# First matrix of the last MLP: seven products of block sums for eight

## The chip, the cores and the metric

The kernel runs on one core of a Trainium2 chip. The metric is the device time of one execution in microseconds (us); three runs of the kernel before took 1508.21, 1509.25 and 1509.27 us, so the median is 1509.25 us.

## The reference, cut to what matters

A model of two layers works on 16 meta tokens and 512 tokens of width 1024, in float32. Each layer has a token mixer and an MLP; only the MLP of the second layer is touched:

```python
def sq_relu_mlp(h, w1, w2):
    a = jax.nn.relu(h @ w1)
    return (a * a) @ w2
...
        hn = rms_norm(h, norm_g[l, 2])
        h = h + rms_norm(sq_relu_mlp(hn, mlp_w1[l], mlp_w2[l]), norm_g[l, 3])
    return h[:, N_META:]
```

`w1` is 1024 x 4096 and `w2` 4096 x 1024. In the second layer the MLP sees the 512 tokens only, since the meta tokens are dropped from the output.

## The kernel before, in words

**Float32 by three products.** Every operand of a large product is held as two parts of type float32r: `hi`, a copy in that type, and `lo`, what is left. `three` (L528) issues three matmuls for one k tile of 128 rows: hi hi, hi lo, lo hi. All of them are issued by `mm` (L140), so every matmul has line 140; the instructions of VectorE, ScalarE and GpSimd all come from the wrapper at line 88, and every DMA of the SP queue from line 147.

**Weights.** Weights come in chunks of 1 MB: for the first matrix 1024 rows by 256 columns. `fetch` asks for a chunk on SP's queue (two raw buffers), `prepare` splits it (ScalarE makes `wh`, VectorE `wl`, as two operations of 128x1024 each; three buffers for each of `wh` and `wl`), and `chunk` hands it to a product after preparing the next one and fetching the one after. The order of chunks is the list `plan`.

**The last MLP.** `Stream` holds the input: `st.hs` the stream itself, feature-major (8 tiles of 128 features by 512 tokens), and `half_of` its hi and lo parts times the norm's weights, by halves of 256 tokens. D_FF is worked off in four passes of 1024 (`q`). In each pass `mlp_in` makes 8 tiles of the squared ReLU from four chunks of the first matrix, and then four chunks of the second matrix are multiplied, with tokens on the output's partitions (`gemm_tok`); `out_tokens` adds the passes up in `ys`. In the first pass the leading two chunks are worked off by `gemm_lead`, one half of the tokens after the other, while the residual stream is just being made (`residual`); the other 14 chunks go through `gemm_full` (two output tiles of 128, 8 k tiles, three matmuls of 512 columns: 48 matmuls a chunk), and `relu2` evacuates a PSUM bank: ScalarE takes ReLU and square (hi), VectorE squares again and subtracts (lo). PSUM is used in pairs of banks, of which there are three for products (`pair`).

**The token-major stream.** The output needs the stream with tokens on partitions. `by_tokens`, a side task, transposes `st.hs` on TensorE during the first pass and keeps the eight tiles `ht` in SBUF until `finish` adds them.

**What sets the order.** TensorE's and ScalarE's instructions and the DMAs on SP's queue run in the order in which the program writes them. VectorE's and GpSimd's are put in order by the framework's planner, from a simulated timeline (`unpin`). Side tasks are generators: `spawn` gives one a due time on a clock that counts matmul columns, and `tick`, called between matmuls, runs the step that has waited longest. All small tiles come from one pool of 61 units of 128x528 (`U`).

Of the kernel before, what the change touches and what calls it, by code (L numbers as in the profile page):

```python
# [10 lines left out]
F32 = mybir.dt.float32  # L11
F32R = mybir.dt.float32r
# [61 lines left out]
def trunk(ctx, tc, io, out, dbg=None):  # L74
# [3 lines left out]
    class Engine:  # L78
        """an engine whose instructions keep the order they are written in where pinned is set"""
# [69 lines left out]
    # ------------------------------------------------------------ constants  # L149
# [16 lines left out]
    # ------------------------------------------------------------ input  # L166
# [47 lines left out]
    # ------------------------------------------------------------ accurate small functions  # L214
# [29 lines left out]
    def small_parameters():  # L244
# [13 lines left out]
        # softplus(-lam) * 4  # L258
# [13 lines left out]
        # softmax over the layers, its first row  # L272
# [9 lines left out]
    def s5_parameters():  # L282
        """S5: discretised transition, its powers, and z = (abar - 1) / a"""
# [61 lines left out]
        # nre = 1 - Re(abar), a_re = -ea  # L345
# [23 lines left out]
    # ------------------------------------------------------------ side work, interleaved with the main products  # L369
# [18 lines left out]
    def due():  # L388
        """the step of the side work that has waited longest, of those that have what they wait for"""
        return min((e for e in sides if e[2] is None or e[2]()), key=lambda e: e[0], default=None)  # L390

    def tick():
        """such a step if its time has come, and another where work is late"""
        for late in pace[1:]:
            e = due()
            if e and e[0] <= clk[0] - late:
                run(e)
# [8 lines left out]
    # ------------------------------------------------------------ weight stream  # L406
# [3 lines left out]
    def weights(w, r0, c0, kt=KT, eng=None, order=""):  # L410
        """order: which of rows (r) and columns (c) come as S5 has its features, in each tile (c g) for (g c)"""
        plan.append((w, r0, c0, kt, eng, order))

    def halves(n, kt):
        """the first chunks come in two parts"""
# [15 lines left out]

    def fetch(i):
        while state["dma"] <= min(i, len(plan) - 1):
            n = state["dma"]
            w, r0, c0, kt, _, order = plan[n]
            cw = CW * KT // kt
            raw = pr.tile([P, kt, cw], F32, tag="raw", name=nm("raw"))
# [11 lines left out]
    def prepare(i):  # L449
        fetch(i)  # L450
        while state["split"] <= min(i, len(plan) - 1):
# [48 lines left out]
    for l in range(2):  # L500
# [13 lines left out]
        for q in range(4):  # L514
            for i in range(4):
                weights(w1s[l], 0, q * D + CW * i)
# [11 lines left out]
    def three(o, wc, k, j, x, a, b):  # L528
        """one k tile of w^T x in three products of float32r parts"""
# [14 lines left out]
    def gemm(ps, wc, j, xs, cut, first=True, last=True, k0=0, n=KT):  # L544
        """accumulates w^T xs for the columns of cut in a PSUM pair"""
# [7 lines left out]
    def gemm_tok(o, wc, xs, c0, n, ks=range(KT), k0=0):  # L553
        """accumulates xs^T w for a block of columns of xs; w starts with k tile k0"""
# [9 lines left out]
    def meta_parts(xs):  # L564
        """hi and lo of the meta tokens side by side, as one stationary operand for each k tile"""
# [7 lines left out]
    def gemm_meta(o, wc, xm):  # L573
        """xs^T w for the meta tokens: what hi gives above what lo gives with the high part of w"""
# [7 lines left out]
    def meta_rows(u):  # L582
        """a side task: adds the two parts"""
# [5 lines left out]
    def gemm_full(ps, wc, j0, xs, c0, n=KT):  # L589
        """w^T xs for two tiles of w and 512 columns, a PSUM bank for each tile"""  # L590
# [6 lines left out]
    def gemm_wide(pss, wc, xs, cut, n=KT, j0=0):  # L597
        """two tiles and their halves side by side, for operands whose last tiles come late"""
# [6 lines left out]
    def split_halves(i):  # L605
        """the split of chunk i in two parts, the k tiles of its first half first"""
# [9 lines left out]
    def gemm_lead(chunks, xs, cut, ready, evac, early=None, lag=5.0):  # L616
        """two chunks, one half of the columns after the other, each tile of xs used as soon as it is there"""
# [3 lines left out]
        for h in range(2):  # L621
# [7 lines left out]
            for i in range(2):  # L629
                if i == len(wcs):  # L630
# [12 lines left out]
    def gemm_trail(parts, cut, evac, after):  # L643
        """the last chunks, one half of the columns after the other, so that what follows can start on the first"""
# [37 lines left out]
    # ------------------------------------------------------------ norms  # L682
# [1291 lines left out]
```

## Time and profile before

| | us |
|---|---|
| median of three runs | 1509.25 |
| span of the profiled execution, first to last instruction | 1506.2 |
| TensorE busy | 1452.0 |
| VectorE busy | 869.8 |
| ScalarE busy | 565.8 |
| GpSimd busy | 509.9 |

The profile is of one execution; its own time is known as the span, and the median of the runs is 3.05 us longer than that. PE is TensorE, DVE VectorE, ACT ScalarE, POOL GpSimd, SP the engine that issues the DMAs. A matmul's listed duration contains its way through the array, so the distance between starts tells the rate. The last MLP's first product starts at 1129.3 us, and its last matmul at about 1497 us.

### The profile page before, as it was taken

To read this page: it belongs to the slowest core of one execution; us is meant where nothing else is said; L and a number is where in the kernel's file an instruction comes from. 1 tells how busy PE (TensorE), PEld (TensorE's weight loads), DVE (VectorE), ACT (ScalarE), POOL (GpSimd) and SP (SyncE) were. 2 spreads that over 40 slices of the span, in tenths; PEclk is the share of its full clock that TensorE was granted. 3 is DMA by queue.
4 is the path that set the end of the run, shared out by engine and by line. 5 is a ranking of instruction groups with operands and counts; after the bars stand their busy time and mean duration, and the time that the engine had idled before them with its cause. 6 is when DMAs were issued, how large, how long until landed. Compare 5 with 4: busy or idle time off the path is not lost.

```text
span 1506.2 us, 24782 instructions
## 1 busy us (share of the span) xinstructions
PE 1452.0 (96%) x10216; PEld 1346.0 (89%) x10216; DVE 869.8 (58%) x1321; ACT 565.8 (38%) x935; POOL 509.9 (34%) x627
## 2 busy tenths in 40 slices
PE   7999998999999999999999889998999999999997
PEld 6998898889989999999999889988798888888887
DVE  5787699664279635345344937659469424334245
ACT  6344373443227222233233532344436324133133
POOL 3535264232122985629401444435123000000004
PEclk9999999999999999999999999999999999999999
DMA  7315012303155343423344285630142222413121
GB/s 245 100 57 156 29 61 73 107 33 132 61 149 161 99 148 114 137 84 107 121 135 166 86 194 189 170 86 29 57 154 67 102 84 84 140 56 132 64 84 56
DMA packets 154464, 162.38 MB, mean 108 GB/s; under 512 B 30292, under 2 KB 126912, under 8 KB 154336
## 3 DMA queue, kind: packets, MB, share of 16 engines
q1 hardware_dynamic: 151824, 160.23, 33.5%
q8 instruction: 80, 1.31, 0.3%
q10 hardware_dynamic: 2176, 0.52, 0.2%
q14 instruction: 32, 0.26, 0.1%
q0 software_dynamic: 352, 0.05, 0.0%
HBM read 136.89 MB, written 20.64 MB: 105 GB/s over the span
## 4 chain that ended last, share of the span: by engine, by line
PE 78%; DVE 15%; ACT 3%; issue 2%; DMA 1%; POOL 1%; SPq 0%; DVEq 0%; ACTq 0%; POOLq 0%
PE m L140 43%; PE wo L140 6%; PE v L140 4%; PE trail L140 3%; PE lead L140 3%; DVE wl L88 2%; PE gt L140 2%; PE av L140 2%; DVE m L88 2%; PE i L140 2%; PE f L140 2%; DVE z L88 1%; PE hs L140 1%; PE ms L140 1%; DVE rt L88 1%
## 5 line engine op out<-in xcount | busy, mean ns | idle before, releaser
L88 DVE TENSOR_TENSOR wl<-raw,wh 128x1024 fp32r<-128x1024 f32 (+1 forms) x204 | 265.8, 1344 | 82.3 <-ACT wh L88 81.7
L88 ACT CAST wh<-raw 128x1024 fp32r<-128x1024 f32 (+1 forms) x228 | 219.1, 1016 | 81.4 <-PE m L140 54.3
L140 PE MATMUL m<-nh,wh 128*128 128x264 f32 (+1 forms) x672 | 216.7, 323 | 0.0
L140 PE MATMUL m<-nl,wh 128*128 128x264 f32 (+1 forms) x672 | 215.6, 321 | 0.0
L140 PE MATMUL m<-nh,wl 128*128 128x264 f32 (+1 forms) x672 | 215.3, 320 | 0.0
L88 DVE TENSOR_TENSOR mr<-mr 128x528 f32<-128x528 f32 (+3 forms) x72 | 48.0, 668 | 184.3 <-ACT ah L88 183.0
L140 PEld LDWEIGHTS m<-nh,wh 128*128 128x128 f32 x672 | 126.4, 188 | 10.4 <-issue 0.7
L140 PEld LDWEIGHTS m<-nh,wl 128*128 128x128 f32 x672 | 126.4, 188 | 9.6
L140 PEld LDWEIGHTS m<-nl,wh 128*128 128x128 f32 x672 | 126.5, 188 | 9.3
L140 PE MATMUL m<-ah,wh 128*128 128x264 f32 x448 | 128.3, 286 | 0.0
L140 PE MATMUL m<-al,wh 128*128 128x264 f32 x448 | 127.3, 284 | 0.0
L140 PE MATMUL m<-ah,wl 128*128 128x264 f32 x448 | 127.3, 284 | 0.0
L88 POOL TENSOR_TENSOR y<-y,gb 128x256 f32<-128x256 f32 (+1 forms) x12 | 11.5, 966 | 313.0 <-ACT junk L88 312.6
L88 ACT ACTIVATE mr<-m 128x528 f32<-128x528 f32 (+1 forms) x56 | 33.6, 599 | 200.2 <-PE m L140 188.1
L140 PE MATMUL m<-wh,ah 128*128 128x512 f32 (+1 forms) x288 | 106.7, 370 | 0.0
L140 PE MATMUL m<-wh,al 128*128 128x512 f32 (+1 forms) x288 | 106.0, 368 | 0.0
L140 PE MATMUL m<-wl,ah 128*128 128x512 f32 (+1 forms) x288 | 105.9, 368 | 0.0
L88 POOL TENSOR_TENSOR sq<-sq,sq 128x264 f32<-128x264 f32 (+2 forms) x38 | 37.1, 980 | 177.9 <-ACT sq L88 175.1
L140 PEld LDWEIGHTS m<-ah,wh 128*128 128x128 f32 x448 | 84.3, 188 | 0.7 <-issue 0.7
L140 PE MATMUL lead<-nh,wh 128*128 128x264 f32 (+1 forms) x256 | 77.4, 302 | 7.3 <-ACT nh L88 6.6
L140 PEld LDWEIGHTS m<-al,wh 128*128 128x128 f32 x448 | 84.3, 188 | 0.0
L140 PEld LDWEIGHTS m<-ah,wl 128*128 128x128 f32 x448 | 84.2, 188 | 0.0
(446 smaller groups left out, 4192.1 us busy)
## 6 DMA issues: line engine op xcount, KB each, us to landing
raw<-mlp_w SPq DMA_DIRECT2D x64, 1024.0 KB, 5.3
raw<-w_in_ab SPq DMA_DIRECT2D x18, 1024.0 KB, 5.0
raw<-w_in_cd SPq DMA_DIRECT2D x10, 1024.0 KB, 8.3
raw<-w_out_ab SPq DMA_DIRECT2D x8, 1024.0 KB, 5.3
hr<-hsp SPq DMA_DIRECT2D x16, 264.0 KB, 6.0
hsp<-h SPq DMA_DIRECT2D x8, 264.0 KB, 4.0
rbs<-rb SPq DMA_DIRECT2D x16, 132.0 KB, 2.2
hsp<-m SPq DMA_DIRECT2D x8, 264.0 KB, 7.5
```

The lines of the kernel that those rows point to most:

```text
L88: i = f(*a, **k)
L140: return tc.keep_in_program_order(T.matmul(o, lhsT=l, rhs=r, start=a, stop=b))
```

## The change

Fourteen of the 16 chunks of the first matrix (all but the leading two) go through a new class `Seven`. It takes chunks in pairs. Each chunk of 1024 rows by 256 columns is seen as 2 x 2 blocks: two halves of its rows (`kh`) and two of its columns (`j`); the stream is seen as 2 x 2 blocks of four feature tiles by 256 tokens. One level of Strassen's scheme, in Winograd's form, needs seven block products in place of eight. A block product is four k tiles, three matmuls of 256 columns each.

- `feed` makes the stationary operands, up to eight ahead of the product in work. Per chunk: four sums or differences of blocks (128x512) on GpSimd; seven copies to `hi` on ScalarE; the `lo` parts of five on VectorE and of two (P3, P4) on GpSimd. Four operands share one of the three weight buffers. The next raw chunk is fetched after the operand P4 is made.
- `moving_sums`, a side task that starts when the residual is complete, makes the four sums of stream blocks, per feature tile: a difference on GpSimd, a scaled copy on ScalarE, three scaled differences on VectorE, four copies on ScalarE and four subtractions on VectorE, all of 256 columns. They stay in SBUF.
- `run` issues the products for the two chunks of a pair side by side, in the order P1, P2, P6, P7, P4, P5, P3. `seven_evac` adds the products in SBUF: per pair one copy on ScalarE, seven additions on VectorE that read PSUM, and for four output tiles the squared ReLU; two of them take three ScalarE operations and one on VectorE, the other two a fused operation on VectorE, a copy on ScalarE and a subtraction on VectorE.
- In the first pass there is one pair, fed during the second half of `gemm_lead`; in the others there are two, the first eight operands of which are fed during the last chunk of the second matrix of the pass before.
- The hi and lo parts of the stream are packed by halves, two feature tiles side by side.
- The token-major stream is written to DRAM (`htd`, eight transfers) as it is made, and read back (eight transfers) after the first matrix of the last pass.

The diff, cut to this (comments that were only taken out are not shown):

```diff
+    def fetch_blocks(src):
+        raw = pr.tile([P, KT, CW], F32, tag="raw", name=nm("raw"))
+        for kh in range(2):
+            dma(out=raw[:, 4 * kh : 4 * kh + 4], in_=src[:, 4 * kh : 4 * kh + 4])
+        return {(j, kh): raw[:, 4 * kh : 4 * kh + 4, j * P : j * P + P] for j in range(2) for kh in range(2)}
...
+            if "S" in order:
+                raws[n] = fetch_blocks(w[r0 : r0 + D, c0 : c0 + CW].rearrange("(k p) c -> p k c", p=P))
+                state["dma"] += 1
+                continue
...
-        while state["split"] <= min(i, len(plan) - 1):
+        while state["split"] <= min(i, len(plan) - 1) and "S" not in plan[state["split"]][5]:
...
-                weights(w1s[l], 0, q * D + CW * i)
+                seven = l == 1 and (q > 0 or i > 1)
+                weights(w1s[l], 0, q * D + CW * i, order="S" if seven else "")
...
+    SEVEN = ("P1", "P2", "P6", "P7", "P4", "P5", "P3")
+    class Seven:
+        def __init__(self, n0, pairs):
+            self.n0, self.pairs, self.n = n0, pairs, 14 * pairs
+            self.fed, self.ops, self.s = 0, {}, {}
+        def feed(self, upto):
+            while self.fed < min(upto, self.n):
+                i = self.fed
+                pair_, o = divmod(i, 14)
+                prod, e = SEVEN[o // 2], o % 2
+                n = self.n0 + 2 * pair_ + e
+                fetch(n)
+                a, s = raws[n], self.s
+                if i % 4 == 0:
+                    self.group = [pw.tile([P, 4, 4, P], F32R, tag=t, name=nm(t)) for t in ("wh", "wl")]
+                if prod == "P1":
+                    for m in (1, 2):
+                        s[e, m] = U("ws")[:, :512].rearrange("p (k c) -> p k c", k=4)
+                    G.tensor_tensor(s[e, 1], a[1, 0], a[1, 1], ADD)
+                    G.tensor_tensor(s[e, 2], s[e, 1], a[0, 0], SUB)
+                elif prod == "P2":
+                    G.tensor_tensor(a[1, 0], a[1, 0], a[0, 0], SUB)
+                elif prod == "P7":
+                    G.tensor_tensor(s[e, 2], a[0, 1], s[e, 2], SUB)
+                src = s[e, {"P5": 1}.get(prod, 2)] if prod in ("P3", "P5", "P6") else a[
+                    {"P1": (0, 0), "P2": (0, 1), "P4": (1, 1), "P7": (1, 0)}[prod]]
+                hi, lo = (g[:, i % 4] for g in self.group)
+                S.copy(hi, src)
+                (G if prod in ("P3", "P4") else V).tensor_tensor(lo, src, hi.bitcast(F32), SUB)
+                self.ops[i] = hi, lo
+                self.fed += 1
+                if prod == "P4":
+                    fetch(n + 2)
+                if prod == "P3":
+                    del raws[n]
+                    state["split"] += 1
+        def run(self, xops, evac):
+            last = (self.n + 3) // 4 - 2
+            for i in range(self.n):
+                self.feed(i + 8 - i % 4 if i % 4 == 0 else i + 8)
+                if i == 4 * last:
+                    prepare(self.n0 + 2 * self.pairs)
+                pair_, o = divmod(i, 14)
+                prod, e = SEVEN[o // 2], o % 2
+                if e == 0:
+                    ps = pair("p7")
+                ops, (hi, lo) = xops(prod), self.ops.pop(i)
+                for k in range(4):
+                    three(ps[:, e, :256], (hi, lo), k, 0, ops[k], k == 0, k == 3)
+                    if k % 2:
+                        tick()
+                if e:
+                    evac(pair_, prod, ps[:, :, :256])
+            state["use"] += 2 * self.pairs
...
+                if h and more is not None:
+                    more(4 * i + 4)
...
-            gemm_lead([(w1s[l], 0, CW * i) for i in range(2)], st, cut, st.ready, evac)
+            more = None
+            if l == 1:
+                seven[0] = Seven(state["use"] + 2, 1)
+                more = seven[0].feed
+            gemm_lead([(w1s[l], 0, CW * i) for i in range(2)], st, cut, st.ready, evac, more=more)
+        if l == 1:
+            until(lambda: len(moving[4]) == 4)
+            seven[0].run(lambda prod: moving_of(st, prod), seven_evac(a2))
+            return a2
...
-            if cut is MAIN:
-                ps = pair("m1")
-                gemm_full(ps, wc, 0, st.xs, 0)
-                for j in range(2):
-                    r, hi, lo = U("mr"), U("ah", F32R), U("al", F32R)
-                    relu2(ps[:, j, :], r[:, :512], hi[:, :512], lo[:, :512], 512)
-                    a2.append((hi, lo))
-                continue
...
+    seven, moving = [None], {n: [] for n in (1, 2, 3, 4)}
+    def moving_sums(st):
+        yield lambda: st.ready[1]
+        fst, snd = slice(0, 256), slice(256, 512)
+        for c in range(4):
+            if c % 2 == 0:
+                units = [(U("th", F32R), U("tl", F32R)) for _ in range(4)]
+            cs = slice((c % 2) * 256, (c % 2) * 256 + 256)
+            parts = [tuple(u[:, cs] for u in p) for p in units]
+            t, t_ = U("t5"), U("t5")
+            t1, t2, t3, t4 = t[:, fst], t[:, snd], t_[:, fst], t_[:, snd]
+            h0, h1 = st.hs[c], st.hs[c + 4]
+            g0, g1 = ng(st.l, st.n, c), ng(st.l, st.n, c + 4)
+            G.tensor_tensor(t1, h0[:, snd], h0[:, fst], SUB)
+            yield 0.5
+            S.activation(t1, t1, AF.Copy, scale=g0)
+            V.scalar_tensor_tensor(t2, h1[:, snd], g1, t1, MUL, SUB)
+            V.scalar_tensor_tensor(t3, h0[:, fst], g0, t2, MUL, SUB)
+            V.scalar_tensor_tensor(t4, h1[:, fst], g1, t2, MUL, SUB)
+            yield 1.0
+            for n in (2, 3, 1, 4):
+                (hi, lo), t = parts[n - 1], (t1, t2, t3, t4)[n - 1]
+                S.copy(hi, t)
+                V.tensor_tensor(lo, t, hi.bitcast(F32), SUB)
+                moving[n].append((hi, lo))
+            yield 0.5
+    def moving_of(st, prod):
+        n = {"P5": 1, "P6": 2, "P7": 3, "P4": 4}.get(prod)
+        if n:
+            return moving[n]
+        k0, h = {"P1": (0, 0), "P2": (4, 0), "P3": (4, 1)}[prod]
+        return [st.half_of(k0 + k, h) for k in range(4)]
+    class Halves:
+        def __init__(self, *parts):
+            self.parts = parts
+        def __getitem__(self, at_):
+            c0, c1 = at_[1].start, at_[1].stop
+            return self.parts[c0 // 256][:, c0 % 256 : c0 % 256 + c1 - c0]
+    def seven_evac(a2):
+        u, done = {}, {}
+        def both(t):
+            return t[:, :512].rearrange("p (e w) -> p e w", e=2)
+        def square(j, h, r, fused):
+            hi, lo = U("ah", F32R)[:, :512], U("al", F32R)[:, :512]
+            if fused:
+                V.scalar_tensor_tensor(r, r, 0.0, r, ALU.max, MUL)
+                S.copy(hi, r)
+            else:
+                S.activation(r, r, AF.Relu)
+                S.activation(hi, r, AF.Square)
+                S.activation(r, r, AF.Square)
+            V.tensor_tensor(lo, r, hi.bitcast(F32), SUB)
+            done[j, h] = hi, lo
+        def evac(pair_, prod, ps):
+            def plus(dst, src):
+                u.setdefault(dst, U("mr")[:, :512])
+                V.tensor_tensor(both(u[dst]), ps, both(u[src]), ADD)
+            if prod == "P1":
+                u.clear()
+                u[2] = U("mr")[:, :512]
+                S.copy(both(u[2]), ps)
+            elif prod == "P2":
+                plus(0, 2)
+                square(0, 0, u.pop(0), False)
+            elif prod == "P6":
+                plus(2, 2)
+            elif prod == "P7":
+                plus(3, 2)
+            elif prod == "P4":
+                plus(1, 3)
+                square(1, 0, u.pop(1), False)
+            elif prod == "P5":
+                plus(3, 3)
+                plus(2, 2)
+                square(1, 1, u.pop(3), True)
+            elif prod == "P3":
+                plus(2, 2)
+                square(0, 1, u.pop(2), True)
+                for e in range(2):
+                    es = slice(e * 256, e * 256 + 256)
+                    for j in range(2):
+                        a2.append(tuple(Halves(*(done[j, h][p][:, es] for h in range(2))) for p in range(2)))
+        return evac
...
-    st = Stream(1, 2, MAIN, packed=False)
+    st = Stream(1, 2, MAIN)
+    spawn(moving_sums(st))
...
-    ht = []
+    ht, htd = [], dram("htd", [4, 2, P, 512])
...
-                ht.append(u)
+                dma(out=htd[tt, e], in_=u[:, :512])
...
+        if q == 3:
+            for tt in range(4):
+                for e in range(2):
+                    ht.append(U("ht"))
+                    dma(out=ht[-1][:, :512], in_=htd[tt, e])
...
+                ahead = q < 3 and i == e == 1
+                if ahead:
+                    seven[0] = Seven(state["use"], 2)
+                    seven[0].feed(4)
...
+                    if ahead and tt == 1:
+                        seven[0].feed(8)
```

## Rows read from the trace of the kernel before

**Rows 1.** The page: span, and busy time of each engine with its share.
```profile
span 1506.2 us, 24782 instructions
PE 1452.0 (96%) x10216; PEld 1346.0 (89%) x10216; DVE 869.8 (58%) x1321; ACT 565.8 (38%) x935; POOL 509.9 (34%) x627
```

**Rows 2.** The chain of waits: start, us, engine, tile, line, count.
```profile
1159.31 36.04 PE m L140 x156
...
1239.14 249.54 PE m L140 x1140
```

**Rows 3.** Busy time by stretch: length, PE, PEld, DVE, ACT, POOL, clock, DMA share, GB/s.
```profile
1130.00:1140.00 10.00, 7.81 (x41) 6.85 (x42) 9.37 (x21) 6.84 (x18) 1.74 (x2) 0.83 0.07 14
1140.00:1160.00 20.00, 19.82 (x164) 19.49 (x163) 19.54 (x35) 12.42 (x32) 8.87 (x10) 1.00 0.27 93
1160.00:1180.00 20.00, 20.00 (x89) 16.25 (x88) 11.93 (x17) 9.47 (x19) 3.79 (x4) 1.00 0.26 93
...
1340.00:1360.00 20.00, 20.00 (x88) 16.31 (x87) 9.90 (x12) 8.48 (x12) 0.00 (x0) 1.00 0.20 75
```

**Rows 4.** Timeline, TensorE, 512 columns: start, us, instruction; first and last of 71.
```profile
1159.14 0.40 PE L140 MATMUL m<-nh,wh 128*128 128x512 f32 x1
...
1175.29 0.39 PE L140 MATMUL m<-nl,wh 128*128 128x512 f32 x1
```

**Rows 5.** Timeline, TensorE, 256 columns: first and last of 65.
```profile
1091.12 0.28 PE L140 MATMUL wo<-ycl,wh 128*128 128x256 f32 x1
...
1098.66 0.28 PE L140 MATMUL wo<-ych,wl 128*128 128x256 f32 x1
```

**Rows 6.** Groups by form, VectorE, 1168 to 1470: busy us, mean ns, idle before.
```profile
L88 DVE TENSOR_TENSOR wl<-raw,wh 128x1024 fp32r<-128x1024 f32 x54 | 63.4, 1219 | 30.5 <-ACT wh L88 30.5
L88 DVE TENSOR_TENSOR al<-mr,ah 128x512 fp32r<-128x512 f32 x28 | 19.4, 692 | 1.0
...
L88 DVE TENSOR_TENSOR y<-m,y 128x512 f32<-128x512 f32 x18 | 11.6, 686 | 33.0 <-PE m L140 33.0
```

**Rows 7.** Groups by form, ScalarE, 1241 to 1290.
```profile
L88 ACT ACTIVATE ah<-mr 128x512 fp32r<-128x512 f32 x8 | 5.1, 632 | 0.3
```

**Rows 8.** Groups by form, GpSimd, 1100 to the end.
```profile
L88 POOL TENSOR_TENSOR y<-y,gb 128x512 f32<-128x512 f32 x4 | 5.1, 1294 | 305.5 <-ACT junk L88 305.5
```

**Rows 9.** Timeline, GpSimd, 1475 to 1483.
```profile
1476.19 2.55 POOL L88 TENSOR_TENSOR y<-y,gb 128x512 f32<-128x512 f32 x2 [3.02 <-ACT junk L88]
1479.15 1.26 POOL L88 TENSOR_TENSOR y<-y,gb 128x256 f32<-128x256 f32 x1 [0.41 <-POOL y L88]
1482.53 0.74 POOL L88 TENSOR_TENSOR y<-y,gb 128x256 f32<-128x256 f32 x1 [2.11 <-ACT junk L88]
```

**Rows 10.** Timeline, VectorE: a chunk's split alone, and one at the end.
```profile
1174.38 2.35 DVE L88 TENSOR_TENSOR wl<-raw,wh 128x1024 fp32r<-128x1024 f32 x2
...
1477.80 3.70 DVE L88 TENSOR_TENSOR wl<-raw,wh 128x1024 fp32r<-128x1024 f32 x2
```

**Rows 11.** Timeline, VectorE, entry of the last MLP, 1147 to 1172.
```profile
1147.30 3.24 DVE L88 SCALAR_TENSOR_TENSOR nl<-m,vecs,nh 128x256 fp32r<-128x256 f32 x8
1150.58 0.42 DVE L88 TENSOR_TENSOR mr<-mr 128x256 f32<-128x256 f32 x1
...
1153.77 2.35 DVE L88 TENSOR_TENSOR wl<-raw,wh 128x1024 fp32r<-128x1024 f32 x2
1156.04 2.73 DVE L88 TENSOR_TENSOR sq<-sq,sq 128x256 f32<-128x256 f32 x3
...
1162.28 2.35 DVE L88 TENSOR_TENSOR wl<-raw,wh 128x1024 fp32r<-128x1024 f32 x2
...
1171.72 0.69 DVE L88 TENSOR_TENSOR mr<-mr 128x512 f32<-128x512 f32 x1 [4.43 <-ACT ah L88]
```

**Rows 12.** Timeline, TensorE, after the gap ahead of 1137.53.
```profile
1138.32 0.41 PE L140 MATMUL lead<-nh,wl 128*128 128x256 f32 x1
1138.53 0.41 PE L140 MATMUL lead<-nh,wh 128*128 128x256 f32 x1
```

**Rows 13.** DMA issues from 1100 (KB each, us to landing), and SP's timeline.
```profile
raw<-mlp_w SPq DMA_DIRECT2D x31, 1024.0 KB, 5.1
...
1138.25 0.38 SPq L147 DMA_DIRECT2D raw<-mlp_w  x1
```

More of the change, by code (lines that the diff above doesn't have):

```diff
@@ L614, in split_halves @@
             yield
-    def gemm_lead(chunks, xs, cut, ready, evac, early=None, lag=5.0):
+    SEVEN = ("P1", "P2", "P6", "P7", "P4", "P5", "P3")
[52 more added lines that the diff above has]
+            state["use"] += 2 * self.pairs
@@ L618, in gemm_lead @@
+    def gemm_lead(chunks, xs, cut, ready, evac, early=None, lag=5.0, more=None):
         wcs = [chunk(*chunks[0], 0)]
```

## The prediction

> **What bounds the kernel now.** I read the page's header first, then the chain of waits, then busy time by stretch, then single instructions. TensorE is busy 1452.0 of 1506.2 us [rows 1]. The chain ends in one unbroken piece of TensorE work: `m` products from 1159.31 on, and from 1239.14 for another 249.54 us, apart from the few transposes of the token tiles in between [rows 2]. By stretch [rows 3], TensorE is full from 1160 to the last few microseconds, at a granted clock of 1.00. VectorE uses 9.90 of 20 us, ScalarE 8.48 and GpSimd nothing in a typical stretch of the first matrix (1340 to 1360). So inside the four passes (one quarter of D_FF each) only fewer matmul microseconds help, and there is room on the other engines. The entry is different: from 1140 to 1160 VectorE is busy 19.54 of 20 us. There VectorE sets the pace, and any work added to it is late.
>
> **What TensorE saves.** A chunk of the first matrix was 48 matmuls of 512 columns. Their starts go from 1159.14 to 1175.29 in 70 steps, 0.2307 us each [rows 4], so a chunk is 11.07 us. Now it is seven products of 4 k tiles, three matmuls each, of 256 columns: 84 matmuls. Matmuls of 256 columns in the same order of operands (hi hi, hi lo, lo hi, weights loaded for each) start from 1091.12 to 1098.66 in 64 steps, 0.1178 us each [rows 5]: 9.90 us. That is 1.18 us less per chunk, and 16.5 us in 14 chunks. It is not an eighth of the time (19.4 us), since two steps of 256 columns cost 0.2356 us against 0.2307 for 512.
>
> **What the passes pay elsewhere.** Per pair of chunks (19.8 us of TensorE) there are 14 operands (seven products, two chunks), each 128x512. ScalarE makes 14 high parts and 9 evacuation steps, 23 x 0.632 [rows 7] = 14.5 us: it fits. VectorE makes 10 low parts, 7 additions that read PSUM, 2 fused squares and 4 low parts of the result: 23 x 0.69 [rows 6] = 15.9 us, where two chunks took 8 x 0.69 + 4 x 1.22 = 10.4 before. GpSimd, idle before, makes 8 sums of blocks and 4 low parts: 12 x 1.29 [rows 8] = 15.5 us.
> Passes 2 to 4 each have one run of two pairs, 39.6 us. Eight of its 28 operands are fed ahead, during the last chunk of the second matrix, where VectorE has little to do. That leaves VectorE 46 - 8 = 38 operations, 26.2 us, and the split of the next chunk, 2 x 1.22: 28.7 us. GpSimd keeps 24 - 8 = 16 operations, 20.7 us. Taken alone both fit in 39.6 us.
> They don't run alone. At the end of the kernel two VectorE subtractions of 1024 elements took 3.70 us where the same two took 2.35 undisturbed [rows 10], while GpSimd was busy for 0.94 + 1.26 = 2.20 us of that time, its own 256-element product taking 1.26 instead of 0.74 [rows 9]. So a microsecond of GpSimd beside VectorE work on two SBUF operands costs VectorE about 0.61. Of its 28.7 us in a run, 19.0 are of that kind (24 x 0.69 + 2.4), 48% of the run: 0.61 x 20.7 x 0.48 = 6.1 us more. VectorE is then at 34.8 of 39.6 us. It stays under TensorE on average, but the second pair has most of the feeding and the split, so there it will be behind for a while. Three PSUM pairs (two products, 5.7 us, of slack) and up to 8 operands ahead absorb most of this. The ends are 0 (all absorbed) and 9.8 us a run (28.7 + 20.7 - 39.6, the two engines never at work together). I take 1.3 us a run, near the lower end, since the row shows partial overlap and the buffers are several products deep: 3.9 us.
> The next pair's raw weights are asked for only after GpSimd's low part for product P4 of the same chunk. A transfer takes 5.1 us to land [rows 13]; asked for some 3 to 6 us into a pair of 19.8 us, it is there with about 8 us to spare. ScalarE's queue, whose order is fixed, waits on it with evacuation steps behind it; if the cover goes, the price is a part of 5.1 us per pair. I take 0.
>
> **What the entry pays.** In the first pass the seven products start behind the leading two chunks, at 1159.14. P1 and P2 use stored operands and take 48 x 0.1178 = 5.7 us, so at 1164.8 TensorE wants P6, whose moving operand is a sum of stream blocks. For all these sums VectorE gets 12 scaled differences and 16 low parts of 256 columns, 28 x 0.42 [rows 11] = 11.8 us, and they can't start before the residual is done. From 1147.30 on VectorE has the low parts of the stream (3.24 us, [rows 11]), then 25 of those 28 operations (10.5 us) and 6 low parts of weights (4.1) before the last tile of P6's operand is there: 1165.1 if nothing disturbs it. GpSimd adds 4 differences of 0.74 and 6 block sums of 1.29 in the same time, 10.7 x 0.61 = 6.5 us: 1171.6. If the evacuation of the lead's first half (3.2 us, from 1150.58 to 1153.77) stays ahead of it: 1174.8. The two chunk splits there (1153.77 and 1162.28) go, but they are replaced by the feeding. So the wait is 0.3 us at best and 10.0 with the evacuation. With the squares and the evacuation of the second half also in front (2.7 + 3.4) it is 16. I take 7.0, the figure without them. A wait of this size has been followed by half clock here: in the stretch from 1130 to 1140, with a gap in TensorE's work, the clock was 0.83, and 256-column matmuls then started 0.21 us apart instead of 0.118 [rows 3, 12]. I add 1.2 us. The entry costs 8.2 us. The raw data of the two chunks are no obstacle: the second was asked for at 1138.25 [rows 13].
>
> **What costs nothing.** The token-major stream goes to DRAM in 8 transfers and back in 8 more. Both hang on SP's queue, ahead of weight fetches, but a chunk of the second matrix keeps TensorE for 11.07 us and the next two have landed or are on their way; if that cover were gone, the price is one landing, 5.1 us. The packed layout of the stream changes addresses only. The tail is the same.
>
> **The sum.** 16.5 - 3.9 - 8.2 = 4.4 us off the span of 1506.2, so 1501.8. The median lies 3.05 us above the span of the profiled execution; I leave that as it is: 1509.25 - 4.4 = 1504.8 us.
>
> **Rivals.**
> A, the waits are hidden. VectorE has 4.43 us of idle time only at 1171.72, but the order of VectorE's and GpSimd's instructions is planned, so the evacuation and squares could be put behind the sums. Entry 4 us, passes 0: 16.5 - 4 = 12.5, 1496.8 us. Against it: VectorE's 98% in that stretch.
> B, the entry eats the gain. The stream's sums come out behind the evacuations and squares in VectorE's queue, or ScalarE's fixed order keeps PSUM from being read: wait 13, clock 1.2, passes 3.9: 16.5 - 18.1 = -1.6, 1510.9 us. For it: the queue was full from 1147 to 1167 already.
> C, slower: VectorE and GpSimd take turns. If an operation on two SBUF operands and a GpSimd operation never overlap, a run needs 19.0 + 20.7 = 39.7 us of the shared access in 39.6 us, and its second pair 16 x 0.69 + 2.4 + 15.5 = 28.9 in 19.8. TensorE then waits about 5 us a run (9.1 us late, less what the PSUM slack takes up), and at the entry 10.7 x 1 instead of 0.61, 12.4 with the clock: 16.5 - 15 - 12.4 = -10.9, 1520.2 us. It decides from the point where a run loses over 2.8 us, (16.5 - 8.2) / 3. For it: rows 9 and 10 can be read as turns, since the extra 1.35 and 0.52 us nearly make up the 2.20 us of overlap. Against: GpSimd's share is only half of a run.
> The Trainium skill, "SBUF — State Buffer", section "Who interferes with whom", speaks for C: it says that a VectorE instruction with two SBUF inputs and a GpSimd instruction that reads SBUF hold one shared access exclusively, and the later one waits for the whole instruction. By that rule, the trace agrees as far as rows 9 and 10 go, and the sum would be C's.
> D, the products don't run at 0.1178 us: nothing in the rows speaks for it, the order of operands being the same.
>
> **Chances.** Forecast 0.38 (own range 1499 to 1508), A 0.17, B 0.22, C 0.20, D 0.03. About 0.2%, 3 us, can be told from no change. Faster: 0.27 of the forecast's share and A, 0.44. Same: 0.11 of it and 0.14 of B, 0.25. Slower: 0.31, the rest. The range of 1495 to 1518 takes in A and B and the lower half of C.
>
> **What would show it.** In the passes: 256-column `p7` products 0.118 us apart, with gaps under 1.3 us a run; many gaps ahead of products whose releaser is VectorE or a low part would show C, best seen as GpSimd operations far over 1.29 us. At the entry: one gap of about 7 us before P6, VectorE its releaser. A gap ahead of P2 that ScalarE releases would show B. The forecast is wrong if TensorE's gaps after 1159 sum to under 5 or over 16 us.

## The result, and the profile after

The changed kernel takes 1521.2 us (median of 4 runs, 1520.5 to 1523.6), the kernel before on the same chip 1509.3: ratio 1.0081, 95% interval 1.0067 to 1.0095. It is slower by 12 us where 4.4 us less was forecast, and the time lies outside the stated range of 1495 to 1518.

The header and the busy times of the page, which answer to [rows 1]:

```profile
span 1519.2 us, 26277 instructions
PE 1444.8 (95%) x10720; PEld 1365.3 (90%) x10720; DVE 967.0 (64%) x1426; ACT 603.8 (40%) x1032; POOL 641.0 (42%) x715
```

TensorE works 7.2 us less than before and the span is 13.0 us longer, so some 20 us of idle time are new. The chain of waits (start, us, engine, tile, line, count), which in [rows 2] was one unbroken piece of TensorE from 1159.31 on, says where:

```profile
1150.15 9.81 DVE nl L88 x8
1159.96 1.43 DVE t L88
1170.22 1.89 DVE wl L88 x3
1178.26 4.55 DVE wl L88 x4
1185.91 19.17 PE p L140 x144
1205.08 16.70 PE m L140 x72
...
1338.62 19.79 PE p L140 x168
1359.88 1.70 DVE wl L88
...
1424.66 19.80 PE p L140 x168
```

From 1150.15 to 1185.91 the pieces that the chain shows are all VectorE's. Busy time by stretch (length, PE, PEld, DVE, ACT, POOL, clock, DMA share, GB/s), against [rows 3]:

```profile
1150.00:1160.00 10.00, 6.89 (x45) 5.46 (x43) 10.00 (x10) 3.01 (x8) 9.92 (x9) 1.00 0.00 0
1160.00:1170.00 10.00, 4.20 (x21) 4.00 (x22) 9.65 (x23) 7.53 (x21) 1.09 (x1) 0.66 0.01 2
1170.00:1180.00 10.00, 6.77 (x58) 6.56 (x56) 9.76 (x17) 7.22 (x20) 5.56 (x6) 1.00 0.00 0
1180.00:1190.00 10.00, 4.09 (x19) 4.09 (x20) 9.69 (x18) 6.56 (x20) 3.94 (x4) 0.50 0.00 0
...
1360.00:1380.00 20.00, 18.33 (x155) 18.12 (x154) 18.46 (x18) 9.66 (x17) 10.39 (x7) 1.00 0.34 108
```

Between 1150 and 1190 TensorE works 21.95 of 40 us, VectorE 39.1. In a later pass (1360 to 1380) it misses 1.67 of 20.

Split at two marks, the lead's first matmul and the first matmul of the second matrix (before: 1129.32 and 1181.29; after: 1131.90 and 1204.92; the chain's 1205.08 is the listed end of the last `p`), the 13.0 us are: 2.6 ahead of the lead; +21.0 from mark to mark (52.0 to 73.0); -10.7 from there to the end (325.0 to 314.3). The 2.6 are not the change's. Every engine has the same operations in the same order up to there, and over all 14 profiles the lead starts between 1128.7 and 1134.2. So experiments below are read from the lead's first matmul on, and by ratios.

Mark to mark, the lead grew from 29.8 to 41.9 us, and what follows it from 22.1 us (two chunks by eight products) to 31.1, where 19.8 was the price without waits. What happens there, first on VectorE and GpSimd (timeline: start, us, engine, line, instruction, count), against [rows 11]:

```profile
1150.08 9.89 DVE L88 SCALAR_TENSOR_TENSOR nl<-m,vecs,nh 128x256 fp32r<-128x256 f32 x8
...
1172.03 2.73 DVE L88 TENSOR_TENSOR sq<-sq,sq 128x256 f32<-128x256 f32 x3
...
1184.12 1.43 DVE L88 TENSOR_TENSOR tl<-t,th 128x256 fp32r<-128x256 f32 x4
...
1149.83 2.69 POOL L88 TENSOR_TENSOR t<-m 128x256 f32<-128x256 f32 x3
1152.48 1.50 POOL L88 TENSOR_TENSOR ws<-raw 128x512 f32<-128x512 f32 x1
...
1159.64 1.45 POOL L88 TENSOR_TENSOR raw<-raw 128x512 f32<-128x512 f32 x1
```

The eight low parts of the stream, 3.24 us before, last 9.89 us, beside GpSimd's differences and block sums, which follow one another without a pause. The lead's products wait for these low parts (waits: us in total, times, longest), after and then before:

```profile
PE lead L140 <- DVE nl L88: 4.1, 7, 0.9
```

```profile
PE lead L140 <- DVE nl L88: 1.1, 2, 0.9
```

Then ScalarE, whose order is fixed:

```profile
1152.52 0.49 ACT L88 ACTIVATE t<-t,vecs 128x256 f32<-128x256 f32 x1
1161.41 0.41 ACT L88 CAST th<-t 128x256 fp32r<-128x256 f32 x1 [8.40 <-DVE t L88]
...
1164.06 1.54 ACT L88 CAST th<-t 128x256 fp32r<-128x256 f32 x4 [0.65 <-DVE t L88]
1165.51 0.37 ACT L88 ACTIVATE mr<-lead 128x256 f32<-128x256 f32 x1
...
1183.25 0.40 ACT L88 CAST th<-t 128x256 fp32r<-128x256 f32 x1 [3.13 <-DVE t L88]
1183.84 1.02 ACT L88 CAST th<-t 128x256 fp32r<-128x256 f32 x3 [0.18 <-DVE t L88]
1184.76 0.37 ACT L88 ACTIVATE mr<-lead 128x256 f32<-128x256 f32 x1
```

ScalarE stands 8.40 us at a copy of the first stream sum, because VectorE is held on the low parts. Behind that copy stands the first read of the lead's PSUM (1165.51), 33.6 us after the lead's first matmul; before, it came 20.4 us after it (1149.74). The second such read (1184.76) stands behind the fourth tile's copies. TensorE's two longest waits are for these two:

```profile
1166.65 0.58 PE L140 MATMUL lead<-nh,wh 128*128 128x256 f32 x1 [5.78 <-ACT mr L88]
...
1176.49 0.28 PE L140 MATMUL p<-nh,wl 128*128 128x256 f32 x1
1185.91 0.58 PE L140 MATMUL p<-nh,wh 128*128 128x256 f32 x1 [9.14 <-ACT mr L88]
1186.29 0.41 PE L140 MATMUL p<-nl,wh 128*128 128x256 f32 x1
```

The 24 `p` matmuls up to 1176.49 are P1 of both chunks; P2, with stored operands, finds no PSUM. After each gap the granted clock is at 1.2 GHz for a while (0.66 and 0.50 on average in the stretches above; the `p` behind 1186.29 start 0.21 us apart). From start to start, the last 48 lead matmuls take 7.13 us instead of 48 x 0.1178 = 5.65, the 144 `p` 19.01 instead of 16.96: 3.5 us.

### The profile page after: what moved, and what is told of

It reads as the page before. It is cut to its first block, busy times and chain, and to the rows that moved or that the text cites. A ratio compares the mean times of both kernels' runs of the same rounds, so it can differ in the third digit from the quotient of the medians.

```text
span 1519.2 us, 26277 instructions
## 1 busy us (share of the span) xinstructions
PE 1444.8 (95%) x10720; PEld 1365.3 (90%) x10720; DVE 967.0 (64%) x1426; ACT 603.8 (40%) x1032; POOL 641.0 (42%) x715
## 4 chain that ended last, share of the span: by engine, by line
PE 73%; DVE 18%; issue 3%; ACT 3%; DMA 2%; POOL 1%; SPq 1%; DVEq 0%; ACTq 0%; POOLq 0%
PE m L140 33%; PE p L140 8%; PE wo L140 6%; DVE wl L88 3%; PE v L140 3%; PE trail L140 3%; PE lead L140 3%; PE gt L140 2%; PE av L140 2%; DVE m L88 2%; PE i L140 1%; DVE z L88 1%; DVE nl L88 1%; PE hs L140 1%; PE ms L140 1%
## 5 line engine op out<-in xcount | busy, mean ns | idle before, releaser
L88 DVE TENSOR_TENSOR wl<-raw,wh 128x1024 fp32r<-128x1024 f32 (+1 forms) x218 | 293.6, 1387 | 63.4 <-ACT wh L88 62.7
L140 PE MATMUL m<-nh,wh 128*128 128x264 f32 x448 | 128.5, 287 | 0.0
L140 PE MATMUL m<-nh,wl 128*128 128x264 f32 x448 | 127.6, 285 | 0.0
L140 PE MATMUL m<-nl,wh 128*128 128x264 f32 x448 | 127.5, 285 | 0.0
L88 POOL TENSOR_TENSOR wl<-raw,wh 128x1024 fp32r<-128x1024 f32 (+1 forms) x38 | 77.1, 2043 | 86.6 <-ACT wh L88 86.6
L88 DVE TENSOR_TENSOR mr<-mr 128x528 f32<-128x528 f32 (+2 forms) x44 | 29.4, 669 | 88.4 <-ACT ah L88 87.0
L140 PEld LDWEIGHTS m<-nh,wh 128*128 128x128 f32 x448 | 84.3, 188 | 0.8 <-issue 0.7
L140 PEld LDWEIGHTS m<-nl,wh 128*128 128x128 f32 x448 | 84.4, 188 | 0.0
L140 PEld LDWEIGHTS m<-nh,wl 128*128 128x128 f32 x448 | 84.4, 188 | 0.0
L140 PE MATMUL lead<-nl,wh 128*128 128x264 f32 (+1 forms) x256 | 78.1, 305 | 5.6 <-DVE nl L88 5.5
```

The source lines that it names most:

```text
L88: i = f(*a, **k)
L140: return tc.keep_in_program_order(T.matmul(o, lhsT=l, rhs=r, start=a, stop=b))
```

## Experiments

First, one table. "Entry" is from the lead's first matmul to the second matrix's first, "rest" from there to the end of the span, each from the one trace of that kernel, rounded; the ratio is to the kernel before, timed on the same chip.

| kernel | lead + following = entry | rest | ratio (95%) |
|---|---|---|---|
| before | 29.8 + 22.1 = 52.0 | 325.0 | 1 |
| after | 41.9 + 31.1 = 73.0 | 314.3 | 1.0081 (1.0067 to 1.0095) |
| sums_on_vector | 35.1 + 34.7 = 69.8 | 314.3 | 1.0042 (1.0022 to 1.0062) |
| sums_late | 34.7 + 38.5 = 73.3 | 315.7 | 1.0075 (1.0055 to 1.0095) |
| both_moved | 29.7 + 40.2 = 69.9 | 315.4 | 1.0062 (1.0042 to 1.0081) |
| no_low_sums | 42.1 + 29.6 = 71.6 | 314.6 | 1.0070 (1.0051 to 1.0089) |
| both_moved_no_low | 30.2 + 38.5 = 68.8 | 315.4 | 1.0055 (1.0040 to 1.0071) |
| stored_blocks | 29.2 + 26.5 = 55.7 | 314.9 | 0.9951 (0.9937 to 0.9966) |
| plain_first | 36.9 + 23.3 = 60.2 | 315.2 | 0.9985 (0.9974 to 0.9996) |
| plain_first_sums_late | 30.4 + 22.6 = 53.0 | 313.5 | 0.9932 (0.9918 to 0.9946) |
| low_on_vector | 30.2 + 22.6 = 52.8 | 319.1 | 0.9974 (0.9964 to 0.9984) |
| all_on_vector | 29.7 + 22.6 = 52.3 | 311.3 | 0.9912 (0.9898 to 0.9926) |

**Is it turns? before_adds and before_memsets.** By turns is meant that VectorE and GpSimd do not run at the same time: one waits while the other has an operation. To the kernel before, additions on GpSimd beside the low parts, with results that nobody uses; in the second kernel one addition and then 15 memsets of the same size, which write but read nothing. In both the squares of the stream are also written later.

```
+    def extra(st):
+        u = U("xt")
+        for k in range(6):
+            G.tensor_tensor(u[:, :512], st.hs[k][:, :512], gb3[0][:, :512], ADD)
# before_memsets: one such addition, then 15 x G.memset(u[:, :512], 0.0)
```

> The kernel before, with six additions of 128x512 on GpSimd (their results unused) while VectorE makes the low parts of the stream's second half, and the squares written 20 us later so that nothing stands between. Turns: each of the eight low parts waits for one GpSimd operation, they take 9 to 10 us instead of 3.24, and the additions 1.4 us each. Sharing without turns: both are stretched evenly, the low parts to at most 5 us. TensorE's lead gets 3 to 6 us longer by turns.

> As before_adds, with one addition and then 15 memsets of 128x512 on GpSimd (about 0.53 us each, 7.9 us), which write but read nothing. If it is reading that the two engines take turns in, the low parts wait for the one addition only and take 3.3 to 5 us; if any GpSimd work holds VectorE up, they take 7 us or more.

VectorE and GpSimd of before_adds, then of before_memsets (timeline):

```profile
1147.09 9.38 DVE L88 SCALAR_TENSOR_TENSOR nl<-m,vecs,nh 128x256 fp32r<-128x256 f32 x8
...
1146.85 8.54 POOL L88 TENSOR_TENSOR xt<-m,gb 128x512 f32<-128x512 f32 x6
```

```profile
1148.15 4.26 DVE L88 SCALAR_TENSOR_TENSOR nl<-m,vecs,nh 128x256 fp32r<-128x256 f32 x8
...
1147.91 1.44 POOL L88 TENSOR_TENSOR xt<-m,gb 128x512 f32<-128x512 f32 x1
1149.41 8.12 POOL L88 MEMSET xt<- 128x512 f32 x14
```

Six additions of 1.42 us bring the low parts from 3.24 to 9.38 us, one addition and 14 memsets to 4.26, of which the one addition can account. Both runs came out as turns had it. So it is not any work of GpSimd that holds VectorE up, but operations that read SBUF: beside those, a VectorE operation of 0.4 us is held for 1.02 us by a GpSimd one of 1.42 ((9.38 - 3.24) / 6). The Trainium skill, "SBUF — State Buffer", section "Who interferes with whom", says that a VectorE instruction with two SBUF inputs contends with a GpSimd instruction that reads SBUF, and not with one that only writes it; these two runs agree with it. The wait for the whole instruction that the prediction took from there they do not show: it is 1.02 of 1.42 us. The additions cost the lead 4.0 us (33.9 against 29.8) and the memsets 0.5. One run each: 1514.0 and 1510.4 us, beside 1511.1 for before.

**Take the turns away, or move the stream's sums: sums_on_vector, sums_late, both_moved.** The first makes the first pass's block sums on VectorE; the second starts the stream's sums behind the lead, so that their copies no longer stand ahead of the first PSUM reads in ScalarE's order; the third does both.

```
+                B = V if self.pairs == 1 else G          # sums_on_vector
-                    G.tensor_tensor(s[e, 1], a[1, 0], a[1, 1], ADD)
+                    B.tensor_tensor(s[e, 1], a[1, 0], a[1, 1], ADD)
...
-    spawn(moving_sums(st))                               # sums_late
...
             gemm_lead([(w1s[l], 0, CW * i) for i in range(2)], st, ...)
+            if l == 1:
+                spawn(moving_sums(st), 0.0)
```

> Changed kernel, with the four block sums a chunk of the first pass made by VectorE in place of GpSimd (8 operations of about 0.69 us). Theory 1 (the entry is late because of turns between GpSimd's sums and VectorE's low parts of the stream, and because ScalarE's fixed order puts the copies for the stream's sums ahead of the reads of PSUM): the eight low parts take 3 to 5 us instead of 9.8, the entry gets about 5 us shorter, 1515 to 1517 us. Theory 2 (VectorE has too much work at the entry, in whatever order): 5.5 us more on VectorE, 1525 to 1527 us.

> Changed kernel, with the sums of stream blocks written after the lead's evacuations instead of between its products. Theory 1: both waits of TensorE that ScalarE releases (5.8 and 9.1 us) go, a single wait of 8 to 12 us ahead of P6 takes their place, released by VectorE; 1514 to 1518 us. Theory 2: the work is the same and so is the time, 1520 to 1523 us.

> Changed kernel, with the first pass's block sums on VectorE and the stream's sums written after the lead's evacuations: both things that held the lead up are gone. VectorE's queue as the bound: the lead ends within 31 us of its start, as before, but the products wait for the stream's sums as long as they did; 1514 to 1521 us. If the lead's delay was the loss: the products follow at once, 1506 to 1511 us.

Medians 1516.4, 1521.8 and 1521.0 us, against 1510.8 for before in the first two and 1511.1 in the third. Each edit shortens the lead by 7 us, both together bring it back to 29.7. The products take most of it back, 31.1 us after the change and 34.7, 38.5 and 40.2 in these three, so the entry gets 3.2 us shorter at most. sums_on_vector is within the time of its theory 1, but its entry is not 5 us shorter (its six runs spread from 1512.2 to 1521.3 us, and the trace is of one at 1519.9); sums_late takes the time that theory 2 had, and both_moved that of VectorE's queue as the bound. PSUM is held without turns too: in sums_on_vector, where VectorE does the block sums itself and the low parts take 4.72 us, TensorE still waits 3.2 and 11.9 us for the two PSUM reads, as much in all as the 5.8 and 9.1 before. What the products wait for in both_moved (timeline, TensorE, first matmul after each larger gap):

```profile
1174.90 0.39 PE L140 MATMUL p<-th,wh 128*128 128x256 f32 x1 [3.57 <-ACT th L88]
...
1181.15 0.58 PE L140 MATMUL p<-th,wh 128*128 128x256 f32 x1 [4.17 <-ACT th L88]
1183.33 0.58 PE L140 MATMUL p<-tl,wh 128*128 128x256 f32 x1 [1.60 <-DVE tl L88]
...
1188.78 0.58 PE L140 MATMUL p<-tl,wh 128*128 128x256 f32 x1 [0.30 <-DVE tl L88]
```

Now it is P6, tile by tile, waiting for the stream's sums themselves. Early, the sums block PSUM; late, they block P6, with waits of 13.0 us in all.

**Is it VectorE's amount of work? no_low_sums and both_moved_no_low.** The 16 low parts of the stream's sums are left out (the high part stands for both), in the kernel after and in both_moved: 6.7 us of VectorE less.

```
-                units = [(U("th", F32R), U("tl", F32R)) for _ in range(4)]
+                units = [(U("th", F32R),) * 2 for _ in range(4)]
...
                 S.copy(hi, t)
-                V.tensor_tensor(lo, t, hi.bitcast(F32), SUB)
-                moving[n].append((hi, lo))
+                moving[n].append((hi, hi))
```

> Changed kernel, with the low parts of the sums of stream blocks left out (the high part is used in their place, so the products are as many as before): 16 operations of 0.42 us less on VectorE at the entry, 6.7 us. If VectorE's queue decides when the products can run, the entry gets 6 to 9 us shorter, 1512 to 1516 us. If ScalarE's order decides, at most 2 us: 1519 us or more.

> The kernel with both things moved, and without the 16 low parts of the stream's sums (their high parts are used in place of them, so that part of the computation is left out). Theory 1a (the sums are late because VectorE has more to do than time, once ScalarE's order no longer blocks): 16 x 0.42 = 6.7 us of VectorE go, the second matrix starts 5 to 7 us earlier after the lead's first matmul, 63 to 65 us instead of 70.0, and the time is 1514 to 1516 us. Theory 1b (the sums are late by their own chain through GpSimd, ScalarE and VectorE and the place where they start): at most 2 us, 1519 to 1521.

The entry shortens by 1.4 and 1.1 us, and the medians are 1521.0 and 1518.9 us. Of 6.7 us of VectorE's work hardly any was on the path, though VectorE was 98% busy from 1150 to 1190. In no_low_sums it is busy 34.0 of these 40 us and stands idle four times for 1.2 to 1.4 us, waiting for ScalarE. So VectorE's amount of work does not decide; what is left is the chain over GpSimd, ScalarE and VectorE.

**Take the sums out of the entry: stored_blocks.** both_moved, with stored blocks of the stream as moving operands of the first pass where sums belong; the sums are made behind that pass.

```
+            if q == 0:
+                stored = {"P5": (0, 0), "P6": (4, 0), "P7": (0, 1), "P4": (4, 1), ...}
+                seven[0].run(lambda prod: [st.half_of(stored[prod][0] + k, stored[prod][1])
+                                           for k in range(4)], seven_evac(a2))
+                spawn(moving_sums(st), 0.0)
+                return a2
```

> The kernel with both things moved, but in the first pass the five products whose moving operand is a sum of stream blocks use stored blocks of the stream in its place (that part of the computation is changed); the sums themselves are made behind the first pass, for the other three. Theory 1 (what holds the seven products up is that P6 cannot start before the stream's sums exist): the lead stays at about 30 us, the products come down from 40.3 to 20 to 23 us, the second matrix starts 50 to 53 us after the lead's first matmul instead of 70.0, and the time is 1501 to 1505 us. Theory 2 (VectorE's other work at the entry, the feeding of weights and the additions from PSUM, holds them up): the products stay above 30 us and the time above 1511.

1503.1 us against 1510.4, as theory 1 had it, but the products take 26.5 us instead of 20 to 23. The entry falls from 69.9 to 55.7: the sums, wait and work together, held 14.2 us of it. What is left has other releasers (timeline, TensorE, its two gaps after the lead):

```profile
1162.50 0.39 PE L140 MATMUL p<-nh,wh 128*128 128x256 f32 x1 [1.61 <-ACT mr L88]
...
1174.30 0.39 PE L140 MATMUL p<-nh,wh 128*128 128x256 f32 x1 [3.07 <-DVE mr L88]
```

Evacuations and combinations still cost 4.7 us, so even without any wait for sums the seven products do not pay in this pass as it is ordered (26.5 us against 22.1).

**Leave the first pass plain: plain_first, plain_first_sums_late.** The two chunks behind the lead by eight products as before, in matmuls of 256 columns, the seven only in passes 2 to 4; the second also has the sums behind the lead.

```
-                seven = l == 1 and (q > 0 or i > 1)
+                seven = l == 1 and q > 0
...
-        if l == 1:
+        if l == 1 and q > 0:
             until(lambda: len(moving[4]) == 4)
```

> Changed kernel, with the two chunks behind the lead of the first pass done by eight products as before (matmuls of 256 columns); seven products in the 12 chunks of passes 2 to 4 only; the stream's sums stay where they are. Theory 1: no block sums at the entry, so the low parts of the stream take 4 to 5 us, but ScalarE's order still holds PSUM for the copies: a wait of 3 to 6 us is left; 1503 to 1506 us. Theory 2: VectorE has 15 us less to do before pass 2, no wait is left; 1499 to 1501 us.

> As plain_first, with the stream's sums also written after the lead's evacuations. Both theories: no wait of TensorE at the entry; the median falls by 23.5 of the entry's excess less the 2.8 us that the two chunks lose: 1499 to 1502 us, below both kernels. Above 1505 us would mean that passes 2 to 4 lose more than their 4 us once the entry is not late.

1508.2 and 1499.8 us against 1510.8. With the sums in their old place the lead still waits (36.9 us), behind it does not (30.4): 6.5 us for the place of one line. The first misses both ranges by over 2 us, though a wait for PSUM is left as theory 1 had it (3.2 us); the second is within its range and beats both kernels.

**What is left in the passes: low_on_vector, all_on_vector.** On plain_first_sums_late, first the low parts of P3 and P4, then also the block sums of the passes from GpSimd to VectorE.

```
-                (G if prod in ("P3", "P4") else V).tensor_tensor(lo, src, hi.bitcast(F32), SUB)
+                V.tensor_tensor(lo, src, hi.bitcast(F32), SUB)
# all_on_vector: also G.tensor_tensor -> V.tensor_tensor for the four sums of blocks
```

> The version with eight products in the first pass and the sums behind the lead, and in the other passes the low parts of P3 and P4 on VectorE (0.69 us each) instead of GpSimd (1.29). Turns theory (VectorE loses in the passes what GpSimd holds of the shared access): four turns of 1.29 a run of two pairs and more go for 0.69 each, the 2.9 us that the three passes still lose come down to 1 to 2, and the time is 1498 to 1499. Amount theory (VectorE has too much to do in the second pair of each pass): 8 more operations of 0.69 a pass, 1501 to 1504.

> As the version before it, and the sums of weight blocks of the passes on VectorE too, so that GpSimd has nothing in them. Turns theory: no turns are left, each sum costs VectorE 0.69 instead of a turn of 1.29; 1497 to 1499. Amount theory: VectorE needs 54 x 0.69 + 2.4 = 39.7 us in a run of 39.6 and the second pair is late by several us in each pass: 1505 to 1515.

1506.3 and 1497.7 us against 1510.4. Groups of instructions by form in the first 40 us of pass 3 (busy us, mean ns, idle before), first in plain_first_sums_late, then in all_on_vector:

```profile
L88 DVE TENSOR_TENSOR wl<-raw,wh 128x512 fp32r<-128x512 f32 x6 | 8.9, 1493 | 0.0
L88 DVE TENSOR_TENSOR wl<-ws,wh 128x512 fp32r<-128x512 f32 x6 | 7.0, 1165 | 3.2 <-ACT wh L88 3.2
...
L88 POOL TENSOR_TENSOR wl<-raw,wh 128x512 fp32r<-128x512 f32 x4 | 6.1, 1517 | 8.9 <-ACT wh L88 8.9
```

```profile
L88 DVE TENSOR_TENSOR wl<-raw,wh 128x512 fp32r<-128x512 f32 x10 | 6.7, 691 | 2.0 <-ACT wh L88 2.0
L88 DVE TENSOR_TENSOR wl<-ws,wh 128x512 fp32r<-128x512 f32 x10 | 6.6, 688 | 0.0
```

With GpSimd out of the passes VectorE makes 20 low parts in 13.3 us, where 12 took 15.9. In those 40 us VectorE is busy for 34.2 us with 55 operations instead of 32.9 with 35, and TensorE has no gap. The chain of all_on_vector has the two last runs of the first matrix whole, 336 x 0.1180 us:

```profile
1314.66 39.64 PE p L140 x336
1354.30 44.56 PE m L140 x192
1398.86 39.64 PE p L140 x336
```

The rest of the span, 311.3 us, is 13.6 less than before, of 14.2 (12 x 1.18). The half step, low_on_vector, misses the ranges of both theories, that of amount by 2 us: it leaves the eight block sums on GpSimd, and its rest is 5.6 us longer than plain_first_sums_late's. In the stretch just read TensorE waits 1.7 us for ScalarE's and 0.9 for VectorE's `mr`. VectorE's timeline there shows what stands ahead of the second:

```profile
1331.94 5.17 DVE L88 TENSOR_TENSOR wl<-ws,wh 128x512 fp32r<-128x512 f32 x3
1337.04 1.77 DVE L88 TENSOR_TENSOR wl<-raw,wh 128x512 fp32r<-128x512 f32 x1
1338.73 0.68 DVE L88 TENSOR_TENSOR mr<-p,mr 128x512 f32<-128x512 f32 x1
```

Four low parts take 6.9 us beside GpSimd's sums, where four alone take 2.8, and they stand ahead of an addition that reads PSUM. So the turns are there, and the order of VectorE's instructions puts their whole price ahead of a PSUM read; that another order would cost less was not tried. Of all_on_vector against plain_first_sums_late the traces show the gaps gone; the 0.2% between their ratios is within the intervals.

## Why the prediction was wrong

**TensorE's saving: right.** A run of 168 `p` takes 19.79 us, 0.1178 each, as forecast from [rows 5].

**The passes: right in sum.** Forecast 3.9 us; of 14.2 for 12 chunks 10.7 came off the rest, so 3.5 are lost. TensorE's waits there are for low parts of weights on VectorE, and they are gone in all_on_vector, where GpSimd has nothing to do in the passes: turns are how the time is lost, by one trace each. Rival C had 15 for them.

**The entry: the step that failed.** Forecast 8.2 us: "I take 7.0, the figure without them" for the wait ahead of P6, and 1.2 for the clock. Measured: 21.0 longer, plus the 2.4 saved there, 23.4. The 7.0 is the step that failed, by what it left out and by the path that it took.
- "Without them" left out the evacuations and the squares. In the trace VectorE has the evacuation of the lead's first half (from 1166.36) and squares (from 1172.03) ahead of the third and fourth tile of the stream's sums, and the fourth tile's low parts start at 1184.12. So P6's operand would have been some 17 us late (an estimate: 1184.5 against 1164.8 + 2.6 for the later lead), even with nothing else in the way. The prediction named 16 with all of that in front and did not take it.
- The lead was taken to end at 1159.14 as before, and VectorE's delay to matter only from P6 on. But a later VectorE is a later copy on ScalarE, and behind that copy stood the PSUM reads: this path was put at nothing. So the first gap of 5.8 us came inside the lead, and the second, 9.1, ahead of P2. The text named a gap ahead of P2 released by ScalarE as the sign of rival B, and the trace has it; B gave that place 14.2 us with the clock, at a chance of 0.22.
- "From 1147.30 on VectorE has the low parts of the stream (3.24 us)". They took 9.89. The size of this was not missed: the 6.5 us for GpSimd at 0.61 a microsecond stand against 9.89 - 3.24 = 6.65, beside 9.8 us of GpSimd, 0.68 a microsecond. Missed was that the lead's own products wait for these low parts.
- The clock after two gaps cost 3.5 us instead of 1.2.

In numbers, by the distances between TensorE's starts, which are 0.16 us a gap longer than the listed waits: 4.6 us more around the low parts, 5.9 and 9.3 for PSUM, 3.5 for the clock, 23.3 of 23.4. With 5.8, 9.1 and 2.4 us (the passes) the listed waits sum to 17.3 us, over the 16 that the prediction named as the sign that it is wrong.

**The rivals.** C's 1520.2 us lies close to the time by accident: its passes are 11.5 us too dear, its entry 11 too cheap. Its mechanism, turns, is real, but B's does not need it: with the block sums on VectorE the two PSUM waits are 15.1 us in place of 14.9 (sums_on_vector). B's mechanism is the nearest, with an entry of 14.2 for 23.4. Was ScalarE's order the cause, then? Only of the place. With both moved the lead is as before and the entry 69.9 us all the same. What the products of the first pass, in their order, wait for is that four tiles of stream sums have to go from GpSimd to ScalarE, VectorE, ScalarE and VectorE after the residual; taking that chain and its work out gave 14.2 us (stored_blocks). That this is the price of putting seven products right behind the lead is what the prediction did not see: it counted instructions on VectorE, 28 x 0.42, and leaving 16 of them out moved the entry by 1.1 to 1.4 us.

**What stays open.** Whether another order (P3, with a stored moving operand, ahead of P6) could have covered more of the chain, and whether another order on VectorE would have spared low_on_vector its waits; neither was tried. The entries above are of one trace a kernel, so differences of 1 us among them are not sure.

## What to carry to other kernels

A trick that saves matmul time but needs operands made first belongs where TensorE is the bottleneck and its operands were made long before, not right behind a stage that makes them: the same edit lost 12 us with the first pass in it, and won 11 without it and with the sums moved behind the lead. Before moving VectorE work to an idle GpSimd, look whether VectorE runs operations on two SBUF operands in that stretch; here an addition costs VectorE 0.69 us of its own, and one on GpSimd held it for 1.02 (before_adds). And when new instructions enter an engine with a fixed order, list what stands behind them, PSUM reads first.

## What the runs showed of the hardware

Turns go by single operations that read SBUF, not by GpSimd's busy time: six GpSimd additions cost eight VectorE operations 6.14 us (9.38 - 3.24), 1.02 each, while one addition and 14 memsets of 0.58 us beside them cost 1.02 us (4.26 - 3.24), no more than the one addition. The lead, ahead of which every engine has the same operations in the same order, starts up to 5.5 us apart between executions (1128.7 to 1134.2), more than the change's forecast; a difference of two spans has to be split at such a mark before it is read.
